# Layer 0's first modulation in four column chunks, between the first projections, with x and its weights in long lines

## The chip, the cores and the metric

The kernel runs on one core of one Trainium2 chip. A core has five engines that run side by side: TensorE (PE; its weight loads are listed apart as PEld), VectorE (DVE), ScalarE (ACT), GpSimd (POOL) and SyncE (SP). The transfers run on the core's 16 DMA engines; most of them are issued on SP's queue, some on GpSimd's. The metric is the device time of one execution in microseconds (us). Three runs of the kernel before took 2889.49 to 2893.89 us, with a median of 2891.96 us.

## The reference, cut to what matters

The model is a transformer of two layers over 1024 latent tokens and 256 context tokens, each a vector of 1024 numbers. All is float32. Ahead of every sub-layer the tokens are modulated: a vector of shifts and a vector of scales, computed from the condition vectors `c` (latent) and `c_ctx` (context), are applied to each token.

```python
m_lat = split(silu(c) @ ada_w[l] + ada_b[l], 6)       # shift, scale, gate; shift, scale, gate
m_ctx = split(silu(c_ctx) @ ada_w[l] + ada_b[l], 6)
h_lat = x_lat * (1 + m_lat[1]) + m_lat[0]
h_ctx = x_ctx * (1 + m_ctx[1]) + m_ctx[0]
qa, ka, va, qb, kb, vb = split(h @ w_in)              # layer 0: 512, 128, 128, 512, 512, 512 columns
```

In layer 0, `qa`, `ka`, `va` feed a global attention (head group A; q and k are normalised per head and rotated), `qb`, `kb`, `vb` a neighbourhood attention (head group B). An output projection, a gated residual with layer norm and a convolutional feed-forward part follow, then layer 1 in the same manner.

## The kernel before, in words

**Products.** The products of the projections are made from two float32r parts: an operand is split into a high part (an ACT copy, line 112 for weights) and the rest (a DVE subtraction, line 113), and `mm3` (lines 400 to 404) issues three products for one 128-row step. A projection of one token tile of 128 tokens takes 8 steps, 24 products (`prod_tok`, line 406).

**The start.** `ada_first` (line 162) computes the first two of layer 0's six modulation vectors (shift and scale, 2048 columns). It loads the weights as 16 pieces of 512 KB, each 128 rows of 1024 columns, and multiplies each with the two condition vectors in four column strips of the array (line 185). When all 16 are through, the two results are copied, turned by four transposes and added to the bias; only then are shift and scale known for any column. `l0_project` (line 485) loads the tokens' x in pieces of 128 tokens by 512 columns (line 507), turns 128x128 blocks on TensorE (`group`, line 534), scales and shifts them on ACT (line 536) and splits them into `hh` and `hl` (lines 543 to 546). Then k and v of group A (256 columns) are projected for token tiles 0 to 3, beside the transposes of tiles 4 to 7; then q of group A (512 columns) for tiles 0 to 3, beside the transposes of the context tiles; then k and v, and after them q, of tiles 4 to 9; then v of group B for all ten tiles. After this come q and k of group B (`proj_feat`, line 417): twice 12 chunks, each evicted by `ev_feat`.

**The background.** The next four modulation vectors of layer 0 are computed on DVE by a generator, `ada_items` (line 214): eight jobs, each of four loads of 512 KB (two buffers, line 226), 16 DVE operations into two accumulators (one buffer each, lines 231 and 235) and, per accumulator, a sum over the partitions by `ada_sum` (line 318): a cast and a subtraction (lines 321 and 322), two products with a matrix of ones (lines 325 and 326) into the one bank of the PSUM pool `pa`, and an addition of the bias row (line 330). `bg(n)` takes up to n steps of the generator and ends early when a step answers "hold", which `ada_sum` gives between the subtraction and the products. `bg` is called after the token tiles and after each eviction of `proj_feat`; what is left then is run before the stage ends. A second generator, `ada_cols` (line 282), computes two vectors of layer 1 on TensorE between the chunks of `proj_feat` (line 305), with weights loaded on GpSimd's queue. The columns of the convolution weights are turned by four transposes (`conv_cols`, line 1385; line 145), in bank `pa`, after the first v tile. At the end of the stage, columns for two later norms are built (`mod_cols`, line 333).

**What sets the order.** In these stages TensorE runs in the order of the program (`manual_pe`, line 924), while a planner orders the instructions of the other engines and the queues by its own estimate of when each is ready. Later stages are written out for all engines. The attention stage (`attn_ab`, line 927) begins with products `S` (line 763).

## Time and profile before

| | |
|---|---|
| median of three runs | 2891.96 us |
| lowest and highest | 2889.49 and 2893.89 us |
| the profiled execution's own time | 2889.54 us |
| its span, first to last instruction | 2887.5 us |
| mean granted TensorE clock | 0.985 |
| PE, DVE, ACT busy | 95%, 74%, 48% of the span |
| bytes read from and written to HBM | 338.11 and 115.93 MB |

The page of the profile gives busy times per engine, the chain of work that ended last (followed back from the last instruction), and groups of instructions by line. A row of the timeline has a start, a duration (both us), an engine, a line, the operation with its output and input tiles, how many instructions were merged, and in brackets the idle time of the engine before it and what ended it. A clock of 1.00 means that TensorE was granted its full clock.

### The profile page before, as it was taken

The page shows a single profiled execution, that of the slowest core. Times are in us where ns is not written, and L with a number is a line of the kernel's source. Part 1 is how long each engine was busy: PE and PEld are TensorE (multiplying, and loading weights), DVE is VectorE, ACT ScalarE, POOL GpSimd, SP SyncE. Part 2 cuts the span into 40 slices and gives each one's busy share as a digit, 9 for nine tenths or more (in the row PEclk, how much of TensorE's full clock was granted, in tenths as well). Part 3 has the DMA queues.
Part 4 walks back from the last instruction along what each step waited for, and adds up shares of the span by engine and source line. Part 5 has one row for each costly group of instructions (what it writes and reads, how often), then busy time and mean ns, then how long its engine had stood idle before and what let it go on. Part 6 is the DMA issues. An engine that isn't in the chain of part 4 may idle for free.

```text
span 2887.5 us, 45159 instructions
## 1 busy us (share of the span) xinstructions
PE 2753.8 (95%) x16596; PEld 2245.4 (78%) x16596; DVE 2145.7 (74%) x3852; ACT 1381.7 (48%) x2602; POOL 671.6 (23%) x948
## 2 busy tenths in 40 slices
PE   6989999899999999999999999999998999999997
PEld 4877777777789987888888888766677788887886
DVE  4876366667588778888878656677777888887778
ACT  3221155567435654455553344167743555545541
POOL 2611143354451000000001002255543011111002
PEclk8999999999999999999999999999999999999999
DMA  8468711033558663343458525652244355555962
GB/s 263 140 187 277 233 48 34 18 108 113 160 154 244 212 184 104 106 119 112 120 195 293 173 100 171 200 157 83 82 133 163 121 174 178 164 169 199 328 218 92
DMA packets 370661, 457.00 MB, mean 158 GB/s; under 512 B 26168, under 2 KB 265176, under 8 KB 368904
## 3 DMA queue, kind: packets, MB, share of 16 engines
q1 hardware_dynamic: 342952, 369.53, 41.1%
q0 software_dynamic: 24592, 82.89, 8.3%
q8 instruction: 130, 2.13, 0.3%
q10 hardware_dynamic: 2896, 1.70, 0.2%
q14 instruction: 91, 0.75, 0.1%
HBM read 338.11 MB, written 115.93 MB: 157 GB/s over the span
## 4 chain that ended last, share of the span: by engine, by line
PE 67%; DVE 10%; issue 10%; DMA 6%; ACT 4%; POOL 2%; SPq 0%; ACTq 0%; POOLq 0%; DVEq 0%
PE q L1705 7%; PE x L1705 7%; PE y L1705 7%; PE S L763 4%; PE v L1705 4%; PE pv L908 3%; PE T L894 3%; PE mm L402 3%; PE mm L403 3%; PE mm L404 3%; PE d L403 3%; PE d L402 3%; PE d L404 3%; PE dy L2387 3%; PE dx L2387 2%
## 5 line engine op out<-in xcount | busy, mean ns | idle before, releaser
L787 POOL TENSOR_SCALAR P<-P,rin 128x640 f32<-128x640 f32 (+3 forms) x288 | 250.5, 874 | 328.2 <-DVE rin L786 302.6
L1679 DVE TENSOR_TENSOR w<-raw,w 128x512 fp32r<-128x512 f32 x308 | 208.6, 691 | 88.3 <-ACT w L1677 88.2
L112 ACT CAST w<-raw 128x512 fp32r<-128x512 f32 x315 | 183.5, 621 | 170.6 <-PE d L404 66.5
L113 DVE TENSOR_TENSOR w<-raw,w 128x512 fp32r<-128x512 f32 x315 | 204.4, 689 | 73.1 <-ACT w L112 71.0
L763 PE MATMUL S<-k,q 64*128 64x256 f32 (+2 forms) x1824 | 194.2, 338 | 19.1 <-DVE nm L2725 9.4
L784 ACT ACTIVATE P<-P,nm 128x641 f32<-128x641 f32 (+4 forms) x208 | 161.6, 778 | 86.9 <-DVE nm L2725 45.9
L1677 ACT CAST w<-raw 128x512 fp32r<-128x512 f32 x308 | 182.4, 621 | 17.6 <-DVE raw L1684 12.4
L763 PEld LDWEIGHTS S<-k,q 64*128 64x128 f32 x1824 | 137.0, 189 | 56.0 <-issue 19.1
L774 ACT COPY PT<-T 128x512 f32<-128x512 f32 (+1 forms) x250 | 134.6, 565 | 78.3 <-PE T L894 75.4
L908 PE MATMUL pv<-PT,v 128*64 128x128 f32 x2016 | 132.4, 279 | 16.9 <-ACT PT L774 14.5
L894 PE MATMUL T<-ident,P 128*128 128x128 f32 x1008 | 136.7, 283 | 7.7 <-POOL P L787 3.4
L908 PEld LDWEIGHTS pv<-PT,v 128*64 128x64 f32 x2016 | 108.5, 137 | 42.7 <-ACT PT L774 23.3
L402 PE MATMUL d<-w,w 128*128 128x512 f32 x352 | 137.5, 391 | 0.0
L404 PE MATMUL d<-w,w 128*128 128x512 f32 x352 | 137.0, 389 | 0.0
L403 PE MATMUL d<-w,w 128*128 128x512 f32 x352 | 137.0, 389 | 0.0
L772 DVE COPY PT<-T 128x512 f32<-128x512 f32 (+1 forms) x166 | 110.4, 666 | 31.4 <-PE T L894 21.3
L894 PEld LDWEIGHTS T<-ident,P 128*128 128x128 f32 x1008 | 110.4, 142 | 28.0 <-issue 14.0
L786 DVE RECIPROCAL rin<-den 128x1 f32<-128x1 f32 x288 | 46.0, 161 | 113.9 <-ACT P L784 111.2
L1705 PE MATMUL q<-T3h,w 128*128 128x512 f32 x352 | 120.4, 403 | 9.7 <-DVE ug L2342 6.5
L2387 PE MATMUL dy<-w,w 128*128 128x512 f32 x528 | 120.8, 390 | 0.5 <-DVE w L113 0.5
L1705 PE MATMUL q<-T2h,w 128*128 128x512 f32 x352 | 116.1, 391 | 3.0 <-ACT q L2324 2.5
L1705 PE MATMUL v<-T0h,w 128*128 128x512 f32 x352 | 116.7, 393 | 0.0
(445 smaller groups left out, 7767.2 us busy)
## 6 DMA issues: line engine op xcount, KB each, us to landing
raw<-in_up_dram SPq DMA_DIRECT2D x132, 512.0 KB
raw<-in_down_dram SPq DMA_DIRECT2D x59, 512.0 KB
raw<-g SPq DMA_DIRECT2D x44, 512.0 KB
raw<-G SPq DMA_DIRECT2D x38, 512.0 KB
araw<-in_ada_w_dram SPq DMA_DIRECT2D x32, 512.0 KB
raw<-in_w_in_dram SPq DMA_DIRECT2D x28, 512.0 KB
g<-cv POOLq DMA_DIRECT2D x22, 512.0 KB, 3.0
G<-go POOLq DMA_DIRECT2D x44, 256.0 KB, 2.7
```

The source lines that it names most:

```text
L112: nc.scalar.copy(hi, s)
L113: (lo_eng or nc.vector).tensor_sub(lo, s, f32(hi))
L402: nc.tensor.matmul(ps, lh, rh, start=first, stop=False)
L403: nc.tensor.matmul(ps, lh, rl, start=False, stop=False)
L404: nc.tensor.matmul(ps, ll, rh, start=False, stop=last)
L763: self.nc.tensor.matmul(outs[a], q[r, x, qs], k[r, y, ks], start=(i == 0), stop=(i == 2))
L787: nc.gpsimd.tensor_scalar(P[:, :n], P[:, :n], rin, 1.0, ALU.mult, ALU.mult)
L894: nc.tensor.transpose(ps[:, s * 128 : (s + 1) * 128], P[a][:, cols[i + x] : cols[i + x] + 128], self.ident,)
L908: nc.tensor.matmul(O[a * HD : (a + 1) * HD], v_of(a, vts[i + x]), pT[:, s * 128 : (s + 1) * 128], start=(i + x == 0), stop=(i + x == m - 1 ...
L1679: nc.vector.tensor_sub(half(i, 1), src[i], f32(half(i, 0)))
L1705: nc.tensor.matmul(ps, w[:, a, s], r[b][:, k], start=first and k + i == 0, stop=k == 3 and i == 2, skip_group_check=True,)
L2387: nc.tensor.matmul(banks[q][t], ga[i][:, a, c], wd[i][:, b], start=q < 2 and f + k == 0, stop=f == HF - 1 and k == 2, skip_group_check=True,)
```

## The change

The change does these things.

1. The 2048 columns of the first modulation are computed in four chunks j of 512 columns: 256 of the shift and 256 of the scale, those of the same 256 columns of x. The inputs `ada_w` (its first 2048 columns, as `ada0`) and `x` (as `x0` for the first 512 tokens, and with its rows in the order in which the tiles read them) are handed over in an order in which each row of a piece is one line of 4 KB. A piece of weights is 128 rows of two k steps by 512 columns.
2. The start is written out by hand for all five engines in one block: transposes of x, modulation products, turning of a chunk's result (`mod`), splits of the q weights and the q products of token tiles 0 to 3 (`part(j, tile)`: chunk j's two steps, 6 products of 512 columns) alternate. The q products of chunk 3 follow behind the block. Then come k and v of tiles 0 to 3, with the transposes of tiles 4 to 7 inside and between them, then q and, after it, k and v of tiles 4 to 9.
3. The convolution columns are turned in the pool `pt` of three banks, one transpose after each of the v tiles 1, 3, 5 and 7.
4. `ada_sum` holds twice, `ada_cols` waits one step more between its first load and its first product, and `bg` takes one step, not two or three, behind k and v of tiles 4 to 9.
5. The columns of the two later norms are built inside the attention stage. A one-column exponential is run behind the tenth eviction of the k projection. A finished tile's late transposes are issued before, not after, the next tile's eviction.

```diff
-    def ada_first(self, loads):
+    def ada_first(self, tp, wp, pt, acc, m0):
...
+        def load(j, q):
+            wt[j, q] = x = self.t(wp, [128, 2, 512], "wt")
+            nc.sync.dma_start(x, io["ada0"][j, :, 2 * q : 2 * q + 2])
+
+        def products(j, *qs):
+            s = slice(j % 2 * 128, j % 2 * 128 + 128)
+            for q in qs:
+                for k in (2 * q, 2 * q + 1):
                     for c in range(4):
                         nc.tensor.matmul(
-                            ps[h][32 * c : 32 * c + 2, :256], self.cs[:, :, k],
-                            wt[:, c * 256 : (c + 1) * 256], start=k == 0, stop=k == KT - 1,
+                            acc[32 * c : 32 * c + 2, s], self.cs[:, :, k],
+                            wt[j, q][:, k % 2, c * 128 : (c + 1) * 128],
+                            start=k == 0, stop=k == KT - 1,
                             tile_position=(0, 32 * c), skip_group_check=True,
                         )
...
+                if q == 3:
+                    ar[j] = self.t(tp, [128, 128], "ar", bufs=2)
+                    nc.scalar.copy(ar[j], acc[:, s])
+
+        def turn(j):
+            ps = self.t(pt, [128, 4, 128], "tr")[:, 0]
+            nc.tensor.transpose(ps, ar[j], self.ident)
+            nc.vector.tensor_add(
+                m0[:, :, 2 * j : 2 * j + 2],
...
         ps = bank()
         r = load(0)
         yield
+        yield
         for k in range(KT):
...
         nc.vector.tensor_sub(hl[:, 1], acc, f32(hl[:, 0]))
         yield "hold"
+        yield "hold"
         ps = bank()
...
+        E = mybir.EngineType
+        engines = {E.PE, E.DVE, E.Activation, E.SP, E.Pool}
+        with self.tc.manual_schedule(engines=engines), ExitStack() as e0:
+            tp = e0.enter_context(self.pool("p0"))
+            wp = e0.enter_context(self.pool("p0w", bufs=7))
+            acc = self.t(pa, [128, 512], "small")
+            load, products, turn_mod = self.ada_first(tp, wp, pt, acc, m0)
+
+            def mod(j):
+                turn_mod(j)
+                for k in (2 * j, 2 * j + 1):
+                    scaled(0, k, trs.pop(k))
+
+            load_x(0, [0])
+            load_q(0)
+            for q in range(4):
+                load(0, q)
+            load_x(0, [1])
+            load_q(1)
+            for q in range(3):
+                load(1, q)
+            turns(0)
+            products(0, 0)
+            split_q(0)
+            load(1, 3)
+            nc.sync.dma_start(rp, io["rope0"])
+            self.bcast(gq, io["qg"][0])
+            self.bcast(gk, io["kg"][0])
+            products(0, 1)
+            load_x(0, [2])
+            load(2, 0)
...
+            part(0, 0, 1)
+            products(1, 2)
+            load(3, 1)
+            products(1, 3)
+            load(3, 2)
+            part(0, 2)
+            mod(1)
+            tables()
+            part(0, 3)
+            products(2, 0)
+            load(3, 3)
...
+            part(1, 3)
+            products(3, 0, 1)
+            turns(3)
+            load_x(1, [3])
+            products(3, 2, 3)
+            part(2, 0)
+            mod(3)
+            split_k(0)
+            part(2, 1, 2, 3)
+            split_k(1)
...
         with self.manual_pe():
-            load_x(1, 0)
-            load_x(1, 1)
-            wq = self.load_in(w, 0, 512)
             for t in range(4):
-                tok(t, wk, 256, ev_kva)
-                group(1, 2 * t)
+                part(3, t)
+                done(t, psq[t], ev_qa)
+            for t in range(4):
+                tok(t, wk, 256, ev_kva, {4: lambda: group(1, 2 * t)})
                 group(1, 2 * t + 1)
...
             for t in range(4, NT):
-                tok(t, wq, 512, ev_qa)
-                bg(3)
+                tok(t, wk, 256, ev_kva)
+                bg(1)
+            self.conv = []
             for t in range(NT):
                 tok(t, wv, 512, ev_vb)
-                if t == 0:
-                    self.conv = [f() for f in conv]
+                if t in (1, 3, 5, 7):
+                    x = next(conv[t // 4])
+                    if t in (3, 7):
+                        self.conv.append(x)
                 bg(3)
...
             def then2(i):
                 if i >= 2:
                     next(side[1], None)
+                if i == 10:
+                    nc.scalar.activation(self.pad[:, :1], self.mhalf[:, :1], AF.Exp)
...
-            self.m1 = self.mod_cols(
-                st, banks[0], io["ln_g"][0, 0], io["ln_b"][0, 0],
-                [(a[0, 0, 3], a[0, 0, 4]), (a[0, 1, 3], a[0, 1, 4])], "m1",
-            )
...
+            for i, x in ((5, mods), (8, mod1), (9, mod2), (n - 6, first), (n - 4, bias)):
                 ga[i] = (lambda f=ga[i][0], x=x: (x(), f()), ga[i][1])
...
-                    return xs[t]
+                    return io["x"][t * 128 : (t + 1) * 128, :]
```

More of the change, by code (lines that the diff above doesn't have):

```diff
@@ L129, in load_in, with cols_late @@
         return out
-    def cols_late(self, tp, ppool, rows, tag, pool=None, bufs=1):
+    def cols_late(self, tp, ppool, rows, tag, pool=None, bufs=1, bank="small"):
         nc = self.nc
@@ L150, in cols_late, with cols @@
         return make
-    def cols(self, tp, ppool, rows, tag, pool=None, bufs=1):
-        return self.cols_late(tp, ppool, rows, tag, pool, bufs)()
+    def cols(self, tp, ppool, rows, tag, pool=None, bufs=1, bank="small"):
+        return self.cols_late(tp, ppool, rows, tag, pool, bufs, bank)()
     def row128(self, ap):
@@ L189, in ada_first @@
                         )
-            loads()
-            ar = self.t(ap, [128, 2, 256], "ar")
-            nc.scalar.copy(ar[:, 0], ps[0][:, :256])
-            nc.vector.tensor_copy(ar[:, 1], ps[1][:, :256])
-            pt = self.t(pp, [128, 512], "small")
-            for j in range(4):
-                s = slice(j % 2 * 128, j % 2 * 128 + 128)
-                nc.tensor.transpose(
-                    pt[:, j * 128 : (j + 1) * 128], ar[:, j // 2, s], self.ident
-                )
-            m0 = self.t(self.cst, [128, 2, 8, 2], "mod0")
@@ L214, in ada_items @@
+        return load, products, turn
     def ada_items(self, tp, bank, jobs, W=256, nraw=1, nacc=2):
@@ new lines, in l0_project, with load_k, split_k @@
+        wk, kraw = [], {}
+        def load_k(i):
+            kraw[i] = r = self.t(self.raw, [128, 4, 256], "raw")
+            wv = w.rearrange("(k p) n -> p k n", p=128)
+            nc.sync.dma_start(r, wv[:, 4 * i : 4 * i + 4, 512:768])
+        def split_k(i):
+            r = kraw.pop(i)
+            for y in self.split([r[:, :2], r[:, 2:]], 512):
+                v = y.rearrange("p a (k n) -> p a k n", n=256)
+                wk.extend((v[:, 0, k], v[:, 1, k]) for k in range(2))
+        E = mybir.EngineType
@@ L939, in attn_ab, with mods, mod1, mod2 @@
             n = len(ga)
-            for i, x in ((n - 6, first), (n - 4, bias)):
+            late = []
+            def mods():
+                a, io = self.d["ada"], self.io
+                for tag, i, l, p in (("m1", 0, 0, 3), ("m2", 1, 1, 0)):
+                    late.append(self.mod_late(
+                        sp, pt, io["ln_g"][0, i], io["ln_b"][0, i],
+                        [(a[l, v, p], a[l, v, p + 1]) for v in range(2)], tag, 2, "T",
+                    ))
+            def mod1():
+                self.m1 = late[0]()
+            def mod2():
+                self.m2 = late[1]()
+            for i, x in ((5, mods), (8, mod1), (9, mod2), (n - 6, first), (n - 4, bias)):
                 ga[i] = (lambda f=ga[i][0], x=x: (x(), f()), ga[i][1])
```

284 lines of the change are left out of this document (159 added, 125 removed).

## The prediction

> **What bounds the kernel now.** I read the page first, then the busy time of each engine by stretches, then the order of time inside the stretches that the change touches.
>
> ```profile
> span 2887.5 us, 45159 instructions
> PE 2753.8 (95%) x16596; PEld 2245.4 (78%) x16596; DVE 2145.7 (74%) x3852; ACT 1381.7 (48%) x2602; POOL 671.6 (23%) x948
> PE 67%; DVE 10%; issue 10%; DMA 6%; ACT 4%; POOL 2%; SPq 0%; ACTq 0%; POOLq 0%; DVEq 0%
> ```
>
> TensorE is busy 95% of the span and carries two thirds of the chain. So a gain must come from the few places where TensorE waits. The stretches (columns: stretch, length, busy time of PE, PEld, DVE, ACT, POOL, granted clock, DMA share, GB/s) show where they are:
>
> ```profile
> 14.00:24.00 10.00, 6.11 (x64) 0.87 (x64) 0.00 (x0) 0.00 (x0) 0.00 (x0) 0.83 1.03 412
> 24.00:37.00 13.00, 7.89 (x43) 4.62 (x39) 2.47 (x8) 3.27 (x6) 0.00 (x0) 0.63 1.03 288
> 46.00:88.00 42.00, 41.38 (x245) 37.24 (x246) 27.60 (x66) 20.85 (x45) 22.85 (x28) 0.94 0.41 125
> 88.00:150.00 62.00, 61.28 (x352) 53.03 (x351) 58.57 (x105) 18.96 (x47) 41.54 (x49) 1.00 0.60 178
> 150.00:164.00 14.00, 6.34 (x20) 4.35 (x19) 13.64 (x25) 3.25 (x6) 6.78 (x3) 0.63 0.83 250
> ```
>
> Up to 37 us the transfers are the bound (share 1.03) and TensorE only keeps up with them. From 46 to 150 TensorE is full, with VectorE at 94% after 88. From 150 to 164 TensorE is half idle at a clock of 0.63 while VectorE is full. The start in order of time:
>
> ```profile
> 6.18 1.04 PE L185 MATMUL a<-wt,cs 128*2 128x256 f32 x8 [2.68 <-DMA wt<-in_ada_w_dram]
> 19.19 0.62 PE L185 MATMUL a<-wt,cs 128*2 128x256 f32 x8 [0.66 <-DMA wt<-in_ada_w_dram]
> 20.47 1.03 PE L185 MATMUL a<-wt,cs 128*2 128x256 f32 x8 [0.66 <-DMA wt<-in_ada_w_dram]
> 31.55 0.47 PE L534 MATMUL tr<-ident,x 128*128 128x128 f32 x1 [0.45 <-DMA x<-in_x_dram]
> 32.50 0.48 PE L534 MATMUL tr<-ident,x 128*128 128x128 f32 x1 [0.47 <-DMA x<-in_x_dram]
> 46.62 0.58 PE L403 MATMUL mm<-w,hh 128*128 128x256 f32 x1 [2.44 <-DVE w L113]
> 87.12 0.39 PE L404 MATMUL mm<-w,hl 128*128 128x512 f32 x1
> 87.35 0.60 PE L472 MATMUL tr<-ident,q 128*128 128x128 f32 x4
> 87.78 0.60 PE L534 MATMUL tr<-ident,x 128*128 128x128 f32 x4
> 88.14 0.37 PE L402 MATMUL mm<-w,hh 128*128 128x256 f32 x1
> 88.34 0.28 PE L403 MATMUL mm<-w,hh 128*128 128x256 f32 x1
> 88.46 0.28 PE L404 MATMUL mm<-w,hl 128*128 128x256 f32 x1
> ```
>
> A 512 KB piece of modulation weights (lines of 4 KB) takes 1.28 us (19.19 to 20.47); a 256 KB piece of x (lines of 2 KB) 0.95 us. The projection really begins at 46.62. At 88.14 the k/v and q projections of tokens 0 to 3 and all their transposes are done. The pace is 0.23 us a product of 512 columns (87.12 to 87.35), 0.12 us one of 256 (88.34 to 88.46), 0.11 us a transpose (four in 87.35 to 87.78).
>
> **The change, part by part. First, the new start.** It removes nothing from the sum of work; it moves the q projection of tokens 0 to 3 (96 products of 512 columns, 96 x 0.23 = 22 us) under the transfers. Before the last modulation piece lie 21 pieces in lines of 4 KB (4 of x, 16 of weights, the rope table) and 4 of q weights in lines of 2 KB, taken at the price of x, 2 x 0.95. From the first landing at 6.18, so a start of 4.9: 4.9 + 21 x 1.28 + 4 x 1.9 = 39.4, with the two small broadcasts about 40 us. SP issues in written order and must wait for freed buffers, but up to 11 pieces (14 us) lie ahead of the first such wait, so I cost these waits at nothing; without that cover each would add the 2.7 us first-piece wait of row 6.18.
>
> The Trainium skill, "DMA: Bandwidth & Descriptors", section "Bandwidth", puts the limit from HBM at about 358 GB/s per core; the stretch 14 to 24 shows 412. By the page, 13.1 MB would land at 4.9 + 36.6 = 41.5 us, 1.5 us later, and that would leave the sign alone.
>
> On TensorE, until then: 15 pieces of products, now 16 small instructions each instead of 8 wide ones with the same columns, 0.62 us at full clock and 1.03 at half; 24 to 32 transposes; 8 token parts of chunks 0 and 1 at 6 x 0.23 = 1.4 us. From about 18 us (when the second chunk's first piece is there) to 40 that is 11 x 0.62 + 24 x 0.11 + 8 x 1.4 = 20.7 us of 22 at full clock, and nearly twice that at half. So TensorE is almost a second bound, and I allow 2 us of backlog (0 to 8). After the last piece: its products and the turned chunk 1 us, four parts of chunk 2, which cover the chain ACT copy, transpose, VectorE add, scale, split, 5.5 us, four of chunk 3, 5.5 us. q of tokens 0 to 3 ends at 40 + 2 + 12 = 54 us.
>
> The Trainium skill, "TensorE: Matmul & The Clock Gate", part 1, says that the clock falls only after an idle window of some 3.4 us. Row 20.47 disagrees: back to 1.03 us although no wait before it was over 0.66. By the page's rule TensorE would be warm throughout and the 2 us of backlog would not be there.
>
> Then come k/v of tokens 0 to 3 with their transposes: 96 x 0.12 + 32 x 0.11 = 15, 16 transposes of the context 1.8, 16 of the finished q 1.7: 72.5 us, where before stood 88.14. **Gain 15.6 us**; with the backlog at its ends 17.6 and 9.6. VectorE had 27.6 us of work between 46 and 88; without the q weights' eight splits (0.69 each) it needs 22 us in the 25 between 48 and 73, so it fits, barely.
>
> **Second, the conv columns.**
>
> ```profile
> PE small L145 <- DVE cc L147: 4.8, 3, 3.4
> PE small L145 <- DVE abr L330: 2.4, 1, 2.4
> 150.16 0.60 PE L472 MATMUL tr<-ident,q 128*128 128x128 f32 x4
> 160.93 0.63 PE L402 MATMUL mm<-w,hh 128*128 128x512 f32 x1
> 161.36 0.63 PE L403 MATMUL mm<-w,hh 128*128 128x512 f32 x1
> 163.91 0.40 PE L403 MATMUL mm<-w,hh 128*128 128x512 f32 x1
> ```
>
> The four transposes share one PSUM bank with the background modulation and stand in a row behind a VectorE that is late; TensorE goes from 150.6 to 160.93 with 0.9 us of work, then seven products at 0.43. They go to a pool of three banks, one every second token, and fewer background steps are called before them. That frees 9.4 + 1.4; as VectorE was at 94%, some waits may come back on other tiles. I take **9 us** (4 to 11).
>
> **Third, the first column product of layer 1** gets one eviction more between load and use:
>
> ```profile
> 231.84 0.80 PE L305 MATMUL cols<-raw,cs 128*2 128x256 f32 x8 [2.74 <-DMA raw<-in_ada_w_dram]
> ```
>
> **2.7 us** (0 to 2.7): five microseconds of projection now cover it.
>
> **Fourth, what pays for it: the background modulation comes to its end too late.** Each of its 8 jobs (4 loads of 512 KB, 16 VectorE products, two sums) had one hold in each sum; it now has two, and the k/v loop calls one step, not three. A hold ends the call. Counting calls in the code: there are 42; before, the last job is through at the 33rd, nine evictions ahead of the end. After, a job takes 6 calls, and at the last eviction the seventh job's second sum and the whole eighth job are left. They are flushed in TensorE's written order ahead of the first attention product, with one accumulator of each kind and two load buffers, so the flush is a chain:
>
> ```profile
> 272.65 0.49 DVE L231 TENSOR_SCALAR acc<-araw,cs 128x512 f32<-128x512 f32 x1 [2.56 <-DMA araw<-in_ada_w_dram]
> 278.70 0.67 DVE L322 TENSOR_TENSOR ahl<-acc,ahl 128x512 fp32r<-128x512 f32 x1
> 297.85 0.40 PE L326 MATMUL small<-ahl,ones 128*128 128x512 f32 x1
> 345.42 0.28 PE L404 MATMUL mm<-hh,w 128*128 128x256 f32 x1
> 346.81 1.68 PE L763 MATMUL S<-k,q 64*128 64x256 f32 x24 [0.92 <-PE small L145]
> L235 DVE SCALAR_TENSOR_TENSOR acc<-araw,cs,acc x112: 729/746/1791, 97.3 to 292.4; 128x512 f32<-128x512 f32 x112
> L321 ACT CAST ahl<-acc x16: 611/622/644, 111.8 to 294.9; 128x512 fp32r<-128x512 f32 x16
> L322 DVE TENSOR_TENSOR ahl<-acc,ahl x16: 669/672/693, 116.9 to 296.2; 128x512 fp32r<-128x512 f32 x16
> L325 PE MATMUL small<-ahl,ones x16: 394/394/767, 118.1 to 297.6; 128*128 128x512 f32 x16
> 129.83 5.09 DMA araw<-in_ada_w_dram
> 205.79 3.49 DMA araw<-in_ada_w_dram
> 296.63 0.30 SPq L331 DMA_DIRECT2D ada<-abr  x1
> 305.22 0.25 SPq L329 DMA_DIRECT2D abr<-in_ada_b_dram  x1
> ```
>
> From the last projection product: sum 0.7, cast and subtract of the second sum 1.4 (its accumulator comes free), two products 1.3, then the buffer is free and the third load lands after 4.3 (3.5 to 5.1); the last eight products 6.0 less the last one; cast, subtract, sum 2.0; cast, subtract, sum 2.0: 17 us to the first attention product, against 1.4 before. The same piece of chain took 19 us before (278.70 to 297.85), hidden behind the projections, with other VectorE work between. **Loss 15.8 us** (10 to 21), plus a TensorE restarting at half clock, 1.4 us as after 160.93. The cover of this chain was the last nine evictions; it is gone.
>
> **Costed at nothing:** the modulation columns of the later norms, moved into the attention (two small transposes behind two loads, issued three groups ahead, whose products cover them); the load of the exp table, moved from beside the first scores to beside the k projection; x read in a new row order, the same bytes. Without cover each costs once the 0.9 us that row 346.81 waited for such a transpose.
>
> **Sum** against the profiled execution's 2889.54: 15.6 + 9 + 2.7 - 15.8 - 1.4 = 10.1 less, 2879.4. The median of the runs lies 2.4 above that execution, so **2882**. What a measurement of this kernel can tell from no change is about 0.2%, 5.8 us.
>
> **The rivals.** (a) *The flush is hidden.* If the other engines run most of the last job ahead, as at 272.65, where the last job's accumulation started 6 us before the second sum of the job ahead of it (278.70), the 17 us fall away: 2865. Against it: the second accumulator and the load buffers cannot be free before TensorE's last sums. (b) *The start eats its gain.* TensorE at half clock through the interleaved chunks (rows 6.18 and 20.47 are half clock) ends q at 60, and VectorE, full from 88 to 164, gives the conv wait back on other tiles: 9.6 + 4 + 2.7 - 17.2 = -0.9, so 2893, no change. (c) *Slower: the flush stalls on SP.* The two late loads and the bias rows of the sums stand in SP's queue with attention loads and k stores that wait for evictions. Rows 296.63 and 305.22 show such a delay: a bias row was reloaded 8.6 us after the store that freed it. If the two late loads wait 8.6 us each, one behind the other, the flush costs 34 instead of 17 us, and the sum is 2899. It decides from a flush of 27 us on, where the other terms are used up. Against it: at that point the stores in front have their data already.
>
> **How the numbers follow.** Forecast 0.55, with a range of its own of 2872 to 2890; (a) 0.20; (b) 0.15; (c) 0.10. The range for 8 in 10 runs from (a) to near (c): 2864 to 2896. Faster by over 0.2% (below 2886): 0.47 of the forecast and (a), 0.67. Within: 0.22. Slower: 0.11.
>
> **What would show it.** Right: k/v of token 0 begins near 54 us; no gap of TensorE in the v projection; a gap of some 15 us between the last projection product and the first S product, filled by L235-like products on VectorE, with the clock at half behind it. Wrong: no such gap (then 2865), parts of chunk 0 to 2 at 0.43 us a product, or a last modulation piece later than 43 us.

## The result and the profile after

The changed kernel takes **2873.47 us** (median of 4 runs, 2871.38 to 2875.27) against 2892.93 for the kernel before beside it (2889.49 to 2897.90): a ratio of 0.9934, 95% interval 0.9919 to 0.9949. Timed once more with the experiments below it came to 0.9929 (0.9915 to 0.9943). So it is some 20 us faster, and the forecast was 2882. Its profiled execution took 2874.48 us.

The page of the profile of the changed kernel, its span and the busy time of the engines:

```profile
span 2872.6 us, 45400 instructions
PE 2747.7 (96%) x16724; PEld 2244.9 (78%) x16724; DVE 2145.0 (75%) x3852; ACT 1388.0 (48%) x2607; POOL 667.2 (23%) x948
```

TensorE is busy for 6 us less than before, and idle for 9 us less. Where they lie is seen by following the same product through both traces. Rows of TensorE's timeline, first of the kernel before:

```profile
144.67 0.40 PE L402 MATMUL mm<-w,hh 128*128 128x512 f32 x1
214.25 0.39 PE L402 MATMUL mm<-hh,w 128*128 128x512 f32 x1
232.57 0.80 PE L402 MATMUL mm<-hh,w 128*128 128x512 f32 x1
351.30 0.96 PE L894 MATMUL T<-ident,P 128*128 128x128 f32 x3 [0.58 <-DVE m2c L147]
```

And of the changed kernel:

```profile
20.22 0.62 PE L185 MATMUL small<-wt,cs 128*2 128x128 f32 x16
50.90 0.36 PE L405 MATMUL mm<-w,hh 128*128 128x256 f32 x1
69.97 0.48 PE L405 MATMUL mm<-w,hh 128*128 128x512 f32 x1
78.13 0.43 PE L530 MATMUL tr<-ident,x 128*128 128x128 f32 x1 [3.01 <-DMA x<-in_ctx_dram]
136.12 0.51 PE L405 MATMUL mm<-w,hh 128*128 128x512 f32 x1
194.67 0.40 PE L405 MATMUL mm<-hh,w 128*128 128x512 f32 x1
208.93 0.40 PE L405 MATMUL mm<-hh,w 128*128 128x512 f32 x1
214.48 0.62 PE L299 MATMUL cols<-raw,cs 128*2 128x256 f32 x8
322.85 0.28 PE L407 MATMUL mm<-hh,w 128*128 128x256 f32 x1
324.05 0.62 PE L882 MATMUL S<-k,q 64*128 64x256 f32 x6 [0.45 <-DVE qst L465]
336.33 0.79 PE L320 MATMUL small<-ahl,ones 128*128 128x512 f32 x1 [9.13 <-ACT ahl L315]
342.72 1.51 PE L1013 MATMUL T<-ident,P 128*128 128x128 f32 x6 [2.41 <-DVE abr L325]
```

| the product that begins | before | changed | ahead by |
|---|---|---|---|
| the next projection, behind q, k and v of tokens 0 to 3 | 88.14 | 69.97 | 18.2; 16.4 without the 16 context transposes still to do |
| v of token 0 | 144.67 | 136.12 | 8.6 |
| first of the feature projection | 214.25 | 194.67 | 19.6 |
| the 73rd product of the feature projection | 232.57 | 208.93 | 23.6 |
| last of the projections | 345.42 | 322.85 | 22.6 |
| first of layer 0's attention that needs a softmax (T) | 351.30 | 342.72 | 8.6 |

In the kernel before, the first column product of layer 1 stands right ahead of the 73rd product; in the changed kernel it stands one chunk later, at 214.48, and one sum of the background comes later as well. So of the 4.1 us gained between these two rows 2.7 are the wait that is gone, and the rest is mostly work that is still to come.

By the two spans the end is 14.9 us ahead. So the change has three gains and two losses. The gains and one loss, the flush, stand in the forecast; whether by the causes that it gave, the experiments show. The other loss, 7.8 us between 70 and 136 us, is not in it. The flush stands between the first score products S and the first T: six of the products S follow the last projection product after 1.2 us (324.05). Busy time by stretches of the changed kernel, columns as in the prediction:

```profile
10.00:20.00 10.00, 6.96 (x89) 3.55 (x79) 3.18 (x6) 3.38 (x6) 0.00 (x0) 1.00 1.03 408
30.00:40.00 10.00, 10.00 (x130) 7.39 (x129) 5.21 (x8) 4.70 (x9) 5.96 (x6) 1.00 1.04 395
70.00:80.00 10.00, 6.99 (x30) 5.42 (x29) 4.25 (x11) 2.09 (x4) 5.92 (x11) 0.91 0.64 190
80.00:90.00 10.00, 10.00 (x46) 8.01 (x45) 5.61 (x13) 3.65 (x9) 5.80 (x6) 0.92 0.09 28
150.00:164.00 14.00, 14.00 (x65) 11.48 (x64) 8.84 (x18) 3.79 (x8) 0.00 (x0) 1.00 0.74 251
323.00:343.00 20.00, 7.01 (x36) 3.72 (x35) 16.27 (x44) 7.78 (x21) 6.18 (x13) 0.70 0.45 146
```

From 20 us on the start is full and at full pace: the 16 products of a piece take 0.62 us at 20.22. The piece before, at 17.35, still took 1.03 us after a wait of 2.02, although the column of the granted clock has 1.00 there. Behind 17.35 no product waits for a piece: TensorE is the bound of the start then, while the transfers run full ahead of it (share 1.04). The v projection has no gap (14.00 of 14.00, where TensorE was busy for 6.34); before the attention TensorE stands for 13 of 20 us. TensorE's four largest sums of waits from 55 to 137 us:

```profile
PE tr L530 <- DMA x<-in_ctx_dram: 3.0, 1, 3.0
PE small L321 <- DVE ahl L316: 1.8, 1, 1.8
PE small L320 <- DVE abr L325: 1.7, 1, 1.7
PE tr L530 <- DVE qst L465: 1.7, 2, 1.3
```

The first is for the context tiles, loaded only when the last transposes of x have freed a buffer; the next two are for the first job's two sums, met while VectorE is full. These three, 6.4 us, and the 1.7 us of clock that the stretches from 70 to 90 us lack (0.91 and 0.92) are about the unforeseen loss of 7.8. The half clock behind the second sum lies in the v projection. The fourth line, two waits for VectorE's split of q, lies ahead of 69.97.

### The profile page after: what moved, and what is told of

It is laid out like the page before. It is cut to its first block, busy times and chain, and to the rows that moved or that the text cites. A ratio compares the mean times of both kernels' runs of the same rounds, so it can differ in the third digit from the quotient of the medians.

```text
span 2872.6 us, 45400 instructions
## 1 busy us (share of the span) xinstructions
PE 2747.7 (96%) x16724; PEld 2244.9 (78%) x16724; DVE 2145.0 (75%) x3852; ACT 1388.0 (48%) x2607; POOL 667.2 (23%) x948
## 4 chain that ended last, share of the span: by engine, by line
PE 70%; DVE 9%; issue 9%; DMA 5%; ACT 4%; POOL 2%; SPq 0%; ACTq 0%; POOLq 0%; DVEq 0%
PE q L1842 8%; PE x L1842 7%; PE y L1842 7%; PE S L882 4%; PE v L1842 4%; PE pv L1027 3%; PE mm L405 3%; PE mm L407 3%; PE mm L406 3%; PE T L1013 3%; PE dy L2524 3%; PE d L407 3%; PE d L406 3%; PE d L405 3%; PE dx L2524 2%
## 5 line engine op out<-in xcount | busy, mean ns | idle before, releaser
L882 PEld LDWEIGHTS S<-k,q 64*128 64x128 f32 x1824 | 136.9, 187 | 54.5 <-issue 19.1
L903 ACT ACTIVATE P<-P,mc 128x1280 f32<-128x1280 f32 (+1 forms) x80 | 94.7, 1186 | 46.0 <-DVE mc L1148 41.6
```

Of the source, the lines that this page charges most:

```text
L882: self.nc.tensor.matmul(outs[a], q[r, x, qs], k[r, y, ks], start=(i == 0), stop=(i == 2))
L903: nc.scalar.activation(P[:, :m], P[:, :m], AF.Exp, bias=negm, scale=-1.0, accum_out=den)
```

## The experiments

The theory: the changed kernel's time to the attention is the sum of the prediction's terms, and 14 us of the gain are lost again in the flush. The rivals are in each expectation. All ratios are to the kernel before, run beside each; a difference between two ratios is uncertain by some 0.15 to 0.2%, 4 to 6 us. The last column is the start of the first softmax product in the profiled execution, which is sharper for what lies ahead of it (342.72 and 340.59 in two executions of the changed kernel).

| run | median us | ratio | 95% interval | first T |
|---|---|---|---|---|
| changed kernel | 2873.47 | 0.9934 | 0.9919 to 0.9949 | 342.72 |
| once more | 2869.77 | 0.9929 | 0.9915 to 0.9943 | 340.59 |
| one hold | 2878.22 | 0.9950 | 0.9935 to 0.9965 | 340.62 |
| background doubled in the k projection | 2868.14 | 0.9917 | 0.9900 to 0.9934 | 334.72 |
| conv columns together | 2881.53 | 0.9969 | 0.9958 to 0.9979 | 347.32 |
| context buffers | 2869.96 | 0.9925 | 0.9907 to 0.9943 | 334.88 |
| short lines | 2876.12 | 0.9955 | 0.9940 to 0.9969 | 345.82 |
| column product one step earlier | 2873.95 | 0.9952 | 0.9935 to 0.9969 | 338.00 |
| sums in pairs | 2866.79 | 0.9925 | 0.9908 to 0.9941 | 330.50 |
| norm columns at the stage's end | 2887.27 | 0.9998 | 0.9985 to 1.0012 | 349.45 |
| pairs and context buffers | 2860.91 | 0.9898 | 0.9885 to 0.9910 | 328.10 |
| the same, later sums | 2862.67 | 0.9901 | 0.9887 to 0.9914 | 323.78 |
| before, norm columns moved | 2888.48 | 0.9991 | 0.9982 to 0.9999 | 353.41 |

### The flush: one hold

```diff
         yield "hold"
-        yield "hold"
         ps = bank()
```

> The changed kernel with one of the two holds in front of each background sum taken out; nothing else. In the changed kernel the last background job was still undone at the end of the k projection, and 19.9 us lay between the last projection product (322.85) and the first product of layer 0's attention that needs a softmax (342.72), against 5.9 us in the kernel before (345.42 to 351.30). Theory (the second hold is what pushes the job past the end of the stage, and the flush is exposed): the job ends beside the k projection, the stretch falls back to about 6 us, and the time falls by 12 to 16 us, to 2858 to 2862. Rival 1 (attention's start is bounded by something else, its loads for instance): the flush is gone, but the stretch stays above 15 us and the time moves by less than 4 us. Rival 2 (the second hold pays for itself where it stands): each sum now meets ScalarE's and VectorE's split too early and TensorE waits some 3 us at each of seven jobs (1.75 and 1.67 us were seen at the first); the gain of 14 is then eaten, and the time is 2868 to 2880.

The flush is gone: the last projection product begins at 335.10 and the first T at 340.62. But nothing is gained, 0.9950 against 0.9934 and 0.9929. TensorE's waits from 115 to 335 us show where it went:

```profile
PE small L320 <- DVE ahl L316: 6.4, 3, 5.0
PE mm L404 <- ACT w L112: 2.9, 1, 2.9
```

The sums are met before their high and low parts are there (one for 5.0 us), and the weights of the k projection come late as well. The feature projection from its 73rd product on, 113.9 us in the changed kernel (208.93 to 322.85), takes 124.0 (211.12 to 335.10). v of token 0 begins 1.7 us later. Rival 2 holds in its outcome, with fewer and longer waits than it named: the second hold pays for itself, and 12.3 of the flush's 14.4 us came back ahead of it (322.85 to 335.10).

### The flush: the background twice as fast in the k projection only

```diff
                     bg(3)
+                    bg(more)      # 3 in the k projection, 0 in the q projection
```

> The changed kernel, both holds kept, with the background generator called twice instead of once at each eviction of the k projection only, so that its last job ends there. Everything ahead of the k projection is as in the changed kernel. Theory (flush exposed): the same 12 to 16 us as with the single hold, 2858 to 2862, without any change at the earlier sums. Rival (TensorE has no room in the k projection, so that the work comes back as waits there): the stretch to the first softmax product falls to 6 us, but the k projection, 322.85 less some 264, grows by as much, and the time stays within 4 us of the changed kernel. If the single hold gains clearly less than this run, the second hold is worth something where it stands; if both gain the same, it is worth nothing.

Between the two: the first T is 8.0 us earlier, the ratio 0.9917. From the last projection product (329.21) to the first T are 5.5 us instead of 19.9, so 14.4 fall away; the feature projection from its 73rd product on grows by 9.0 (206.29 to 329.21, 122.9). So 5.4 us are the edit's; the other 2.6 of the 8.0 lie ahead of it (206.29 against 208.93), where the code is the same. TensorE's waits from 205 to 335 us for the sums, and the stretches behind the last two of them:

```profile
PE small L320 <- ACT ahl L315: 4.1, 2, 2.1
PE small L321 <- DVE ahl L316: 1.1, 2, 0.7
```

```profile
311.00:312.00 1.00, 1.00 (x9) 0.23 (x9) 0.71 (x2) 0.50 (x1) 0.00 (x0) 0.63 0.85 305
312.00:313.00 1.00, 1.00 (x7) 0.55 (x3) 0.85 (x2) 0.12 (x1) 0.24 (x1) 0.50 0.67 221
313.00:315.00 2.00, 2.00 (x7) 1.56 (x6) 0.00 (x0) 0.00 (x0) 0.29 (x1) 0.58 0.41 76
```

Waits of 5.2 us, and behind the pair at 310 us some 3.4 us at half clock (0.37 + 0.50 + 2 x 0.42 us of clock are missing, 1.71 in all). Sums that TensorE met too early cost more here than their wait.

### The flush: both vectors split before the holds

```diff
-                        yield from self.ada_sum(tp, bank, acc[v], l, v, part, o, W)
+                        hls = hls if v else []
+                        hls.append(self.ada_split(tp, acc[v], W, 2))
+                if bank is not None:
+                    yield "hold"
+                    yield "hold"
+                    for v in vecs:
+                        self.ada_add(tp, bank, hls[v], l, v, part, o, W)
+                        if v == 0:
+                            yield "hold"
```

> The changed kernel with both vectors of a background job split into high and low parts before the holds (two buffers for the parts instead of one) and summed after them, with one hold between the sums: two holds ahead of the first sum as in the changed kernel, but 3 in a job instead of 4, so 5 calls a job instead of 6. Counted out, the last job's second sum alone is left at the end of the k projection. The run with a single hold lost its 14 us of flush again to TensorE's waits for sums that were met too early (5.0 us at 124.67, 1.3 and 0.7 at 224 to 226, and half clock behind them), and the run with doubled calls kept 5 of 14. Theory A (those waits were the price of hurry, not of the flush's work): with the distance kept, the flush goes and no wait comes, 10 to 14 us less than the changed kernel, 2860 to 2864. Theory B (the work itself has no room: the DMA engines are at 0.9 to 1.0 and the jobs' loads and VectorE's products set the pace of the feature projection): waits come back for the weights of the k projection or at the sums, and the gain is 5 us or less, 2868 to 2873.

By the trace theory A: the first T is at 330.50, 12.2 us earlier than in the changed kernel, with the flush down to one sum, and there is no wait for a sum in the feature projection. The last sum in TensorE's timeline, and its waits from 115 to 140 us:

```profile
325.69 0.39 PE L337 MATMUL small<-ahl,ones 128*128 128x512 f32 x1
```

```profile
PE small L336 <- DVE abr L341: 4.3, 1, 4.3
PE small L337 <- DVE ahl L330: 1.7, 1, 1.7
```

The only sums that wait are those of the first job, beside the k/v tokens; there "no wait comes" does not hold. The median is 6.7 us lower, short of the 10 to 14 expected, and the ratio (0.9925) does not stand clear of the changed kernel's; the trace carries the verdict here.

### The conv columns put back

```diff
-                    conv = [self.conv_cols(l, st, pt) for l in range(2)]
+                    conv = [self.conv_cols(l, st, pa) for l in range(2)]
...
-                if t in (1, 3, 5, 7):
-                    x = next(conv[t // 4])
-                    if t in (3, 7):
-                        self.conv.append(x)
+                if t == 0:
+                    for c in conv:
+                        for x in c:
+                            pass
+                        self.conv.append(x)
```

> The changed kernel with the four column transposes of the convolution weights put back as before: all after the v projection's token 0, on the one bank that the background sums use. Theory (the transposes stall TensorE on that bank, and spreading them over three banks freed 9 us): the time from the first v product to the first feature product goes back from 58.6 us to 65 to 70, and the time rises by 7 to 11 us, to 2880 to 2885. Rival (the 9 us came from TensorE's clock and from the loads having more time, not from where the transposes stand): less than 3 us. The measured gain of that stage in the changed kernel was 11.0 us, so 2 us of it may have another source.

The v projection takes 65.5 us instead of 58.6 (135.79 to 201.30), and the time rises by 8.1 us in the median. The theory holds for most of the gain: the stage took 58.6 and 56.9 us in the two executions of the changed kernel, against 69.6 in the kernel before, so 7 to 9 of the 11 to 13 us come back. The other 4 us have a source that was not tried apart; the prediction's term also counted on fewer background steps. TensorE's waits from 135 to 205 us show the same bank, and the granted clock is 0.73 from 144 to 150 us; the changed kernel's v projection has no wait at all:

```profile
PE small L145 <- DVE abr L325: 3.5, 1, 3.5
PE small L145 <- DVE cc L147: 1.4, 3, 0.5
```

### The context tiles in buffers of their own

```diff
-                x[i, j] = r = self.t(xp, [128, D], "x")
+                x[i, j] = r = (
+                    self.t(self.raw, [128, D], "raw") if i == 2 else self.t(xp, [128, D], "x")
+                )
...
         with self.manual_pe():
+            load_x(2)
             for t in range(4):
...
-            load_x(2)
```

The two loads are issued ahead of the last quarter of the q products (45.90 and 49.68 us).

> The changed kernel with the two tiles of context x given buffers that are free some 18 us earlier (those of the raw weights) and their loads issued ahead of the last quarter of the q products. In the changed kernel they were issued at 70.5 and 73.5 us, when the last transposes of x had freed one of four buffers, and TensorE waited 3.0 us for them at 78.13, with a granted clock of 0.91 and 0.92 in the two stretches of 10 us after that. Theory (these buffers caused the part of the start's gain that went lost between the context transposes and the v projection, 7.9 us in all): the wait is gone and with it the half clock, 4.6 us (3 to 6) are gained, 2867 to 2871; the rest of the 7.9 stays, since it lies at 124 to 136 us beside the first background sums. Rival 1 (TensorE is then ahead of VectorE, which was 85 to 100% busy from 100 us on, and waits there instead): below 1.5 us. Rival 2 (the loads collide with the stores of q and k on SyncE's queue or with the weights): slower by 1 to 3 us.

The stretch from 70 to 80 us of this run:

```profile
70.00:80.00 10.00, 10.00 (x50) 8.17 (x48) 7.06 (x18) 3.68 (x7) 8.38 (x14) 1.00 0.32 98
```

From 70 to 80 us of this run TensorE is full and at full clock. v of token 0 begins at 130.89, 5.2 us earlier, and the first T 7.8 us earlier (the other 2.6 us lie behind v of token 0, where the code is the same). The theory holds up to there. The median moves by 3.5 us; behind the first T the profiled execution is 6.6 us slower than the changed kernel's, in code that is the same (see the repeat below).

### Short lines

```diff
-            nc.sync.dma_start(x, io["ada0"][j, :, 2 * q : 2 * q + 2])
+            wa = io["ada_w"][0][:, :2048].rearrange("(k p) (h n) -> p k h n", p=128, h=2)
+            for k in range(2):
+                nc.sync.dma_start(
+                    x[:, k].rearrange("p (h n) -> p h n", h=2),
+                    wa[:, 2 * q + k, :, j * 256 : (j + 1) * 256],
+                )
...
-                    nc.sync.dma_start(r, io["x0"][j])
+                    nc.sync.dma_start(
+                        r.rearrange("p (m d) -> p m d", m=4),
+                        io["x"][:512].rearrange("(m p) d -> p m d", p=128)[:, :, j * 256 : (j + 1) * 256],
+                    )
```

> The changed kernel with the same pieces of x (tokens 0 to 3) and of the modulation weights, in the same order and at the same places, read from the layout that the kernel before read: lines of 1 KB instead of 4 KB, the weights as two transfers a piece. The 8 MB of weights and 2 MB of x ran at 395 to 412 GB/s in lines of 4 KB; lines of 2 KB ran at about 280 in the kernel before. Theory (the long lines carry the new start, which is bound by the transfers): these 10.5 MB take some 38 us instead of 26, k/v of token 0 begin at 62 to 66 instead of 50.9, and the time rises by 8 to 14 us, to 2881 to 2887, so that nearly all of the start's 16 us is the lines'. Rival (TensorE's interleaved work was the second bound, and the pieces came early): below 4 us.

The stretch from 30 to 40 us of this run:

```profile
30.00:40.00 10.00, 9.06 (x97) 6.38 (x96) 4.71 (x7) 4.52 (x8) 5.83 (x6) 1.00 1.09 354
```

The lines of 1 KB run at 354 GB/s, not at 280; k/v of token 0 begin at 54.28, not at 62 to 66, and TensorE's next projection begins at 73.18 instead of 69.97. So 3.2 us of the start's 16.4 are the lines', and the time rises by 2.7 us in the median (by the ratios 6, uncertain by 5). The theory, 8 to 14, falls. What is left, 13 us, is by elimination the new order of the work, in which TensorE rather than the transfers is the bound from 20 us on.

### The column product one step earlier

```diff
         r = load(0)
         yield
-        yield
```

> The changed kernel with one step less between the first load of layer 1's column products and their first use, as before. Theory: TensorE waits 2.7 us again for that load, in the q part of the feature projection, and the clock falls behind the wait, so 2.7 to 4 us more, 2876 to 2878. Rival (the load now finds the queue of GpSimd free, or the background work that is late in the changed kernel has left the transfers room): nothing, within 1.5 us.

The row of this run's timeline in which a column product waits longest:

```profile
246.28 0.62 PE L298 MATMUL cols<-raw,cs 128*2 128x256 f32 x8 [0.46 <-DMA raw<-in_ada_w_dram]
```

Without the extra step the longest wait of a column product is 0.46 us, with no clock drop, and the feature projection up to its 73rd product takes 14.9 us with the column product in it, against 14.3 in the changed kernel, where that product comes later, and 18.3 in the kernel before. The rival holds: the wait went with the new order of the work, not with the step. What in that order brings the load in time was not tried.

### The norm columns put back to the end of the stage

```diff
+self.m1 = self.mod_cols(...)      # behind the flush
+self.m2 = self.mod_cols(...)
-for i, x in ((5, mods), (8, mod1), (9, mod2), (n - 6, first), (n - 4, bias)):
+for i, x in ((n - 6, first), (n - 4, bias)):
```

> The changed kernel with the modulation columns of the two later norms put back to the end of the projection stage, behind the flush, as before (they stand in attention groups 5, 8 and 9 in the changed kernel). The prediction costed the move at nothing. Theory: put back, each meets the store and reload of a row that the flush has only just written, so the flush grows by the two transposes' waits, 2 to 6 us, 2876 to 2880; so the move was worth something beside a late flush though nothing beside an early one. Rival: their loads stand clear of the last store, and the transposes fall into the time in which the first softmax is awaited; within 1.5 us.

They cost far more than either expected: 0.9998, 13.8 us in the median, all that the change had gained. Two rows of this run's TensorE timeline, and then one of its waits between 320 and 380 us:

```profile
344.83 0.34 PE L145 MATMUL small<-ident,rt 48*128 48x48 f32 x1 [1.91 <-DVE abr L325]
348.74 0.31 PE L145 MATMUL small<-ident,rt 48*128 48x48 f32 x1 [3.57 <-DMA rt<-ada]
```

```profile
PE T L1022 <- POOL P L915: 5.4, 2, 4.8
```

In this profiled execution the stretch from the last projection product to the first T grows from 19.9 to 24.2 us (325.22 to 349.45), with the store and reload of the row that the flush has just written inside it. Then GpSimd does four operations for the neighbourhood attention's bias (362.62 to 366.46) ahead of a scaling for which TensorE waits 4.8 us. Another 4 us lie in the feature projection (207.02 to 325.22 takes 118.2 us, not 113.9), with a wait of 4.1 us for k weights that the changed kernel has with 1.4. The edit does not touch the code there, but in this run the planner put the transfers in another order: SP loads two rows of the norms at 194.02 and 194.37 us, which the changed kernel loads at 321.54 and 324.90. So whether these 4 us are scatter or a price of the edit is open. The loss as a whole is not scatter: all ten timed runs (2882.44 to 2895.99) lie above all ten of the changed kernel (2865.51 to 2875.70).

### The same move alone, on the kernel before

```diff
-self.m1 = self.mod_cols(...)      # end of the projection stage
-self.m2 = self.mod_cols(...)
+for i, x in ((5, mods), (8, mod1), (9, mod2), (n - 6, first), (n - 4, bias)):
```

> The kernel before, with one part of the change alone: the modulation columns of the two later norms moved from the end of the projection stage into attention groups 5, 8 and 9. Put back in the changed kernel they cost 13.8 us. Theory (that price comes from their waiting for rows that a late flush has just stored, and from the order that GpSimd gets behind it): here, where the background work ends nine evictions early, only the waits of 0.9, 2.0 and 0.6 us ahead of the first softmax product go: 2 to 4 us less, 0.9986 to 0.9993 of the kernel before. Rival (the move is worth 14 us by itself, and the prediction missed a gain of that size that has nothing to do with the flush): 10 us or more, 0.9965 or less.

0.9991, some 3 us: the theory's size. But its place is not the one expected. From the last projection product to the first T are 5.5 us (347.89 to 353.41) instead of 5.9: TensorE now waits for the softmax instead of the columns. So the gain lies behind the first T, or in the scatter. The rival's 0.9965 lies outside the interval. Beside an early end of the background the move is worth little; beside a late one it is what keeps the change from being worth nothing, though the traces place only a part of the 13.8 us.

### Both edits together, and later sums

> The changed kernel with two of the edits tried before together: both vectors of a background job split ahead of the holds and summed behind them with one hold between (alone: 6.7 us less than the changed kernel), and the two context tiles in buffers that are free early (alone: 3.5 us less). They lie in different stretches (55 to 135 us and 320 to 345 us). Theory (each takes a wait of its own away): the gains add, 10 us, 2861 to 2865. Rival (the background work then has that much less time before the end of the projections, and VectorE and the transfers pace it): only the larger of the two, 2865 to 2869.

2860.91 us, 0.9898: **faster than both kernels by a clear interval**, 31 us below the kernel before and 9 to 13 below the changed one. The time moves as if the two gains added, but at the first T they come to 14.6 us, not 12.2 + 7.8: v of token 0 begins at 136.12, as in the changed kernel, so the first job's sums take back there what the buffers gave. The stretches of the k/v tokens and of the attention's start in this run:

```profile
100.00:135.00 35.00, 27.73 (x190) 25.69 (x189) 31.34 (x61) 13.43 (x31) 19.62 (x27) 0.95 0.77 237
322.00:342.00 20.00, 13.54 (x111) 9.50 (x111) 12.77 (x50) 9.67 (x24) 6.93 (x13) 0.91 0.65 229
```

In front of the attention TensorE works 13.5 of 20 us instead of 7.0. Beside the k/v tokens it loses 7 of 35 us, with VectorE busy for 31. The last edit takes the first job's sums away from there:

```diff
                 tok(t, wk, 256, ev_kva)
-                bg(1)
+                if t < 6:
+                    bg(1)
...
-                    bg(3)         # at each eviction of the feature projection
+                    bg(5)
```

> As the run with both edits together, and in addition no background calls at the last four k/v tokens (so that the first job's sums fall into the v projection) and five steps instead of three at each eviction of the feature projection, which brings the last job to its end at the 11th of 12 evictions of the k part. Theory: the waits of TensorE before the first job's sums (1.75 us at 124.71 and 4.26 at 132.46 in the run with the paired sums), where VectorE is full, go with the half clock behind the second: 5 to 8 us less, 2855 to 2859. Rival (five steps put eight background products in a row in front of the evictions on VectorE, and the waits come back in the feature projection): no gain or up to 5 us more, 2863 to 2868.

The stretch of this run up to v of token 0:

```profile
100.00:129.00 29.00, 26.93 (x199) 25.06 (x197) 26.17 (x48) 12.23 (x27) 15.82 (x20) 1.00 0.79 240
```

TensorE loses 2 of 29 us there, and v of token 0 begins at 128.99, 7.1 us earlier; the feature projection gives 3.4 back (201.18 to 318.25 against 207.43 to 321.10), and the first T stands 4.3 us earlier. The time shows none of it (2862.67, between the theory's range and the rival's): in the trace the waits went as the theory says, and half of the gain went again in the feature projection, as the rival feared.

### The changed kernel once more

> The changed kernel itself, once more. The profiled execution was 6.3 us shorter than the one before between the first softmax product of layer 0 and the end (2529.9 against 2536.2), where no code was changed. Theory (that part is scatter: short waits fall on either side of a clock drop): the same stretch of the new execution is 2532 or longer, and the median is within 2 us of 2873.5. Rival (the new order of the work shifts the later stages reproducibly): again 2529 to 2531.

From the first T to the end this execution takes 2532.9 us, the first one 2529.9 and the kernel before 2536.2. That is the theory's scatter. The median (2869.77), though, is 3.7 us lower than in the first timing, not within 2. Over the eleven profiled executions in which the norm columns have moved and the rest is the changed kernel or an edit ahead of the attention, this stretch is 2532.8 us in the mean, 2527.9 to 2536.5. The later part scatters by some 4 to 5 us to either side, in code that no edit touched. An example, the same place in the changed kernel and in the run with the context buffers:

```profile
593.00:613.00 20.00, 17.89 (x202) 15.45 (x200) 11.49 (x38) 11.39 (x27) 7.69 (x14) 0.91 0.22 74
```

```profile
585.00:605.00 20.00, 17.88 (x192) 15.69 (x190) 10.17 (x33) 10.11 (x23) 8.09 (x13) 0.83 0.22 74
```

The work and the waits are alike, the clock is not: 3.4 us at half clock in the one, 6.8 in the other, and ten products of 202 less done.

## Why the prediction was right, and where it was not

The direction, the flush as the price and the sum up to the attention were right: 10.1 us forecast, 8.6 and 10.7 ahead at the first softmax product in two executions. The terms were not all, and that the sum came so near is in part luck.

**First, the start: right to 72 us, by two errors that cancel, and wrong behind it.** The forecast had 72.5 us against 88.14; 69.97 and 1.8 of transposes to come make 71.8. k/v of token 0 begin at 50.90, not 54: the backlog of 2 us at half clock is not there. But from there to 69.97 are 19.1 us, not the 16.7 of the forecast, with 1.7 us of waits for VectorE, which was to fit "barely". The step that failed is "16 transposes of the context 1.8": it counted TensorE's work and not the load, which waits for a buffer of x. With the half clock and the first job's sums behind it the gain at the v projection is 8.6, not 15.6. The run with own buffers has 5.2 us of it back, the one with own buffers, paired and later sums 7.1: there v begins 15.7 us ahead of the kernel before. Rival (b) saw half of the start's gain lost as well, but by another mechanism, TensorE's half clock from 18 us on, and from 20.22 on that did not occur.

**Second, the conv columns: right for the most part.** 9 us forecast, 11.0 in the stage (8.6 to 19.6); 7 to 9 us come back there when they are put back, 8.1 in the median. The rest has another source.

**Third, the column product: size right, cause wrong.** The wait of 2.7 us is gone, and over the whole feature projection 3.0 us came (131.2 to 128.2 us), but the additional step does not bring them: without it no column product waits for longer than 0.46 us.

**Fourth, the flush: right in kind, with another place and other sizes.** 17.2 us forecast with the cold restart (17 less 1.4 are 15.6, not 15.8), 14.0 measured (5.9 to 19.9). The forecast's sign was a gap ahead of the first S; that gap is not there (324.05), and the flush stands ahead of the first T. It took longer than the 17 us forecast; its price is smaller because in the kernel before 5.9 us, not 1.4, lay ahead of that product, and the softmax work in them now runs inside the flush (VectorE, 326.52 to 330.04). The count of calls was exact: the seventh job's second sum and the whole eighth job are left. VectorE's rows of the flush:

```profile
331.51 4.71 DVE L228 SCALAR_TENSOR_TENSOR acc<-araw,cs,acc 128x512 f32<-128x512 f32 x7
...
341.89 0.68 DVE L325 TENSOR_TENSOR abr<-small,abr 1x512 f32<-1x512 f32 x1 [2.37 <-DMA abr<-in_ada_b_dram]
```

No product in it waits for a load. Of rival (c) only a bias row is left, 2.37 us. Rival (a), the hidden flush, is refuted by the 9.13 us of row 336.33. What the prediction didn't ask is what the same work would cost elsewhere: with one hold most of it comes back.

**"Costed at nothing": wrong for the norm columns.** The cover it named, three groups of products, is there in the attention. The error was to leave out what they would cost at the old place behind a late flush: some 14 us. The load of the exp table was not moved at all: the planner put the one-column exponential, which needs nothing that comes late, at 2.0 us, and the table is loaded beside the first scores as before (346.13 there). Row of ScalarE in the changed kernel:

```profile
324.27 1.28 ACT L903 ACT_TABLE_LOAD   x1
```

**The sum.** By stage 8.6 + 11.0 + 3.0 - 14.0 = 8.6. A start that gained 7 us less, two somewhat better gains and a flush that cost 3.2 us less cancel out; that is luck. The median lies 8.5 us below the forecast all the same. About 3 us may lie in the later stages (2532.8 in the mean against 2536.2 in the one profiled execution of the kernel before), which the prediction held fixed; the move of the norm columns may be their cause, as it was worth some 3 us alone, but single executions scatter by as much. The rest, some 5 us, stays open: one execution of the kernel before is profiled and two of the changed one, and the timed runs of the kernel before alone reach from 2884.90 to 2895.43 in one comparison.

## What to carry to other kernels

When a stage in front gets shorter, count again whether the background work that ran beside it still ends in it; counting generator calls by hand gave the flush here to about 3 us. Be wary of curing a late background by calling it faster, which kept 5 of 14 us here: a sum met too early costs its wait and often some half clock behind it. Making each job need fewer turns at the same distance brought 12 us by the trace. And of each load that a moved step needs, ask which buffer it waits for, not only what its transfer costs.

## What the runs showed of the hardware that was not expected

**Half clock comes in pieces of some 3.4 us, after waits much shorter than that.** The changed kernel, microsecond by microsecond behind the first job's second sum (waits of 1.75 and 1.67 us ahead of the two, at 127.12 and 135.27):

```profile
133.00:135.00 2.00, 0.60 (x6) 0.37 (x4) 1.80 (x6) 1.02 (x5) 1.61 (x4) 1.00 0.92 189
...
136.00:137.00 1.00, 1.00 (x4) 0.75 (x4) 1.00 (x3) 0.33 (x1) 0.84 (x3) 0.62 1.14 345
137.00:138.00 1.00, 1.00 (x4) 0.81 (x3) 0.11 (x1) 0.97 (x3) 0.87 (x2) 0.50 1.15 346
138.00:139.00 1.00, 1.00 (x4) 0.71 (x4) 0.99 (x3) 0.05 (x1) 0.40 (x1) 0.50 0.53 158
139.00:140.00 1.00, 1.00 (x5) 0.82 (x4) 1.00 (x4) 0.57 (x3) 0.00 (x0) 0.67 0.49 145
```

Over 4 us the four rows lack (0.38 + 0.50 + 0.50 + 0.33) = 1.71 us of clock, so 3.4 us at half. The Trainium skill, "TensorE: Matmul & The Clock Gate", part 1, has the clock at half or full, by free-running windows of 3.413 us; that agrees, and it would explain why like waits cost something in one execution and nothing in the next: the wait of 1.75 us here has no half clock behind it (the granted clock is 1.00 from 127 to 136 us), while in the repeat one of 1.54 us, at 127.57, has:

```profile
128.00:129.00 1.00, 1.00 (x7) 1.00 (x6) 0.00 (x0) 0.61 (x2) 0.92 (x3) 0.50 0.95 344
```

The Trainium skill has the half clock come after an idle window; here no wait was over 1.75 us, and TensorE was busy for 0.60 of the 2 us ahead.

**Line length mattered less than the kernel before suggested.** Lines of 1 KB ran at 354 GB/s, those of 4 KB at 395 to 408. The kernel before's x, in lines of 2 KB, needed 0.95 us for 256 KB, 276 GB/s; so something other than the length slowed it, and it was not tried what.
